# A batched A^T B^T matmul on one core: two-bank PSUM copies, no engine block, and the last transposes moved between two halves of a matmul group

## The chip, the cores and the metric

The kernel runs on one core of a Trainium2 chip. The metric is device time in microseconds for one execution; lower is better. Times come from repeated runs of the same program, and a profile comes from one more execution, whose own time is given beside its span (the time from its first to its last recorded instruction).

## The reference

```python
batch, m, k, n = 16, 512, 512, 512
a: (batch, k, m) float32      b: (batch, n, k) float32
np.matmul(a.transpose(0, 2, 1), b.transpose(0, 2, 1)).astype(np.float32)
```

For each of 16 batches the output is A^T B^T, 512 x 512, in float32. Each batch reads 1 MiB of `a` and 1 MiB of `b` and writes 1 MiB of output.

## The kernel before

One batch is one step; there is no tiling over DRAM beyond that. Five engines run their own lists of instructions and meet only at semaphores.

**SyncE (SP)** issues every transfer, all into one queue, in an order written out by hand. In step `i` it issues the load of `b` (line 108), the load of `a` (line 111) and, five steps late (`LAG = 5`), the store of batch `i - 5` (line 123). There are four load buffers for each input and seven output buffers. The load of `b[i]` waits until PE has transposed batch `i - 4` (`turned`), the load of `a[i]` until the first matmul group of batch `i - 4` is done (`summed`), and the store of batch `j` until all groups of batch `j + 1` are done, because that implies that the copies of batch `j` are. The last two stores wait for the copies themselves through `oa_go` and `od_go` (line 122). At the end SP waits for all stores to land (line 125).

**VectorE (DVE)** casts `b` to bfloat16 (`cast`, line 145), moves the transposed `b` from PSUM to SBUF (`turn`, line 151; its source fills two PSUM banks) and copies output groups 0 and 2 from PSUM to SBUF (line 167). Its order inside a batch `i` is: `turn(i + 1)`, copy of group 0, `cast(i + 2)`, copy of group 2. In the last step but one it also does `turn` of the last batch and casts the second half of the last `a` (line 175).

**ScalarE (ACT)** casts `a` to bfloat16 (line 183) and copies output groups 1 and 3 (line 194).

**TensorE (PE)** transposes `b` (8 instructions a batch, line 78; pairs of bfloat16 values are moved as one float32) and does 16 matmuls a batch in four groups `rm` of four (line 90). Each group has its own PSUM bank `o_ps[rm]`, and each group waits until the copy of the same bank in the batch before is done:

```python
def steady(rm):
    take(pe, (od_go, oa_go)[rm % 2])
...
with pe.Fori(0, B // 2 - 1) as _i:
    turn(1)
    multiply(0, 0, steady)
    turn(0)
    multiply(1, 1, steady)
multiply(0, 0, steady)
turn(1)
pe.wait_ge(ac2_go, 1)
multiply(1, 1, last)
```

So batch `i + 1` is transposed ahead of the matmuls of batch `i`, except at the very end, where the transposes of batch 15 come behind all the matmuls of batch 14.

**GpSimd** builds the identity for the transposes and does nothing else.

All of this stands in an `nc.Block()` (line 99) inside a `tc.tile_critical()` (line 42). Each of the two closes with drains and semaphores over the engines.

Of the kernel before, what the change touches and what calls it, by code (L numbers as in the profile page):

```python
# [11 lines left out]
def kernel(  # L12
# [6 lines left out]
    nc = tc.nc  # L19
    P = 128  # L20
    B, K, M = a.shape
    _, N, _ = b.shape
    KO = K // P
    KJ = KO // 2
    MO = M // P
    NO = N // P
    assert B % 2 == 0

    f32 = mybir.dt.float32
    cdt = mybir.dt.bfloat16  # L30
# [3 lines left out]
    a_v = a.rearrange("b (ki ko) m -> b ki ko m", ko=KO)  # L34
    b_v = b.rearrange("b (ni no) k -> b ni no k", no=NO)
    out_v = out.rearrange("b (mi mo) n -> b mi mo n", mo=MO)

    LOADS = 4
    OUTS = 7
    LAG = 5  # L40

    with tc.tile_critical():  # L42
        sb = lambda name, shape, dt: ctx.enter_context(nc.sbuf_tensor(name, shape, dt))
        ps = lambda name, shape, dt: ctx.enter_context(nc.psum_tensor(name, shape, dt))
        sem = tc.alloc_semaphore
        a_sb = [sb(f"a_sb{s}", [P, KO, M], f32) for s in range(LOADS)]
        b_sb = [sb(f"b_sb{s}", [P, NO, K], f32) for s in range(LOADS)]
        o_sb = [sb(f"o_sb{s}", [P, MO, N], f32) for s in range(OUTS)]
        a_bf = [sb(f"a_bf{s}", [P, KO, M], cdt) for s in range(2)]
# [1 line left out]
        bt_sb = [sb(f"bt_sb{s}", [P, KJ, N], f32) for s in range(2)]  # L51
        identity = sb("identity", [P, P], f32)
        bt_ps = [ps(f"bt_ps{s}", [P, KJ, NO, P], f32) for s in range(2)]
        o_ps = [ps(f"o_ps{s}", [P, N], f32) for s in range(MO)]


        a_in = [sem(f"a_in{s}") for s in range(LOADS)]
# [2 lines left out]
        turned = sem("turned")  # L60
# [4 lines left out]
        bt_go = sem("bt_go")  # L65
        ac_go = sem("ac_go")
        ac2_go = sem("ac2_go")
        oa_go = sem("oa_go")
        od_go = sem("od_go")

        def transposes(pe, x, y):

            w = b_bf[x][:].bitcast(f32).rearrange("p no (pk j) -> p no j pk", j=KJ)
            for j in range(KJ):
                for no in range(NO):
                    last = pe.transpose(bt_ps[y][:, j, no, :], w[:, no, j, :], identity[:])  # L78
            last.then_inc(turned, 1)

        def take(pe, s):
            pe.wait_ge(s, 1).then_inc(s, -1)  # L82

        def matmuls(pe, x, y, waits):
            a_r = a_bf[x][:].rearrange("p rk (pm rm) -> p rk rm pm", rm=MO)
            bt_h = bt_sb[y][:].bitcast(cdt).rearrange("p j (n h) -> p j h n", h=2)
            for rm in range(MO):
                waits(rm)
                for rk in range(KO):
                    last = pe.matmul(  # L90
                        o_ps[rm][:],
                        a_r[:, rk, rm, :],
                        bt_h[:, rk // 2, rk % 2, :],
                        start=(rk == 0),
                        stop=(rk == KO - 1),
                    )
                last.then_inc(summed, 1)

        with nc.Block() as block:

            @block.sync
            def _(sp):
                for i in range(B + LAG):
                    s, use = i % LOADS, i // LOADS
                    if i < B:
                        if use:
                            sp.wait_ge(turned, i - LOADS + 1)
                        sp.dma_start(b_sb[s][:], b_v[i]).then_inc(b_in[s], 16)
                        if use:
                            sp.wait_ge(summed, MO * (i - LOADS) + 1)  # L110
                        sp.dma_start(a_sb[s][:], a_v[i]).then_inc(a_in[s], 16)
                    j = i - LAG
                    if j >= 0:


                        if j + 2 < B:
                            sp.wait_ge(summed, MO * (j + 2))
                        else:

                            sp.wait_ge(summed, MO * (B - 1))  # L120
                            for s in (oa_go, od_go):
                                sp.wait_ge(s, 2 * (j + 3 - B))
                        sp.dma_start(out_v[j], o_sb[j % OUTS][:]).then_inc(o_out[j % OUTS], 16)
                for s in range(OUTS):
                    sp.wait_ge(o_out[s], 16 * len(range(s, B, OUTS)))

            @block.gpsimd
            def _(pool):
                pool.memset(identity[:], 0.0).then_inc(id_go, 1)  # L129
                pool.wait_ge(id_go, 1)  # L130
                pool.affine_select(  # L131
                    out=identity[:],
                    in_=identity[:],
                    compare_op=mybir.AluOpType.not_equal,
                    fill=1.0,
                    base=0,
                    pattern=[[-1, P]],
                    channel_multiplier=1,
                ).then_inc(id_go, 1)

            @block.vector
            def _(dve):
                def cast(i):
                    dve.wait_ge(b_in[i % LOADS], 16 * (i // LOADS + 1))
                    dve.tensor_copy(b_bf[i % 2][:], b_sb[i % LOADS][:]).then_inc(bc_go, 1)  # L145

                def turn(i):


                    dve.wait_ge(turned, i + 1)  # L150
                    dve.tensor_copy(  # L151
                        bt_sb[i % 2][:].rearrange("p j (ni no) -> p j ni no", no=NO),
                        bt_ps[i % 2][:].rearrange("p j no ni -> p j ni no"),
                    ).then_inc(bt_go, 1)

                dve.sem_inc(od_go, 2)
                cast(0)
                cast(1)
                turn(0)
                for i in range(B):  # L160
                    if i + 2 < B:
                        turn(i + 1)
                    if i >= OUTS:
                        dve.wait_ge(o_out[i % OUTS], 16 * (i // OUTS))
                    for rm in (0, 2):
                        dve.wait_ge(summed, MO * i + rm + 1)
                        dve.tensor_copy(o_sb[i % OUTS][:, rm, :], o_ps[rm][:]).then_inc(od_go, 1)  # L167
                        if rm == 0 and i + 2 < B:
                            cast(i + 2)
                    if i + 2 == B:  # L170
                        turn(i + 1)

                        s = (i + 1) % LOADS
                        dve.wait_ge(a_in[s], 16 * ((i + 1) // LOADS + 1))
                        dve.tensor_copy(  # L175
                            a_bf[(i + 1) % 2][:, KO // 2:, :], a_sb[s][:, KO // 2:, :]
                        ).then_inc(ac2_go, 1)

            @block.scalar
            def _(act):  # L180
                def cast(i, part=slice(None)):
                    act.wait_ge(a_in[i % LOADS], 16 * (i // LOADS + 1))
                    act.copy(a_bf[i % 2][:, part, :], a_sb[i % LOADS][:, part, :]).then_inc(ac_go, 1)  # L183

                act.sem_inc(oa_go, 2)
                cast(0)
                for i in range(B):
                    if i + 2 < B:
                        cast(i + 1)
                    if i >= OUTS:  # L190
                        act.wait_ge(o_out[i % OUTS], 16 * (i // OUTS))
                    for rm in (1, 3):
                        act.wait_ge(summed, MO * i + rm + 1)
                        act.copy(o_sb[i % OUTS][:, rm, :], o_ps[rm][:]).then_inc(oa_go, 1)  # L194
                    if i + 2 == B:
                        cast(i + 1, slice(0, KO // 2))

            @block.tensor
            def _(pe):
                def steady(rm):  # L200
                    take(pe, (od_go, oa_go)[rm % 2])

                def last(rm):
                    pe.wait_ge((od_go, oa_go)[rm % 2], 1 + rm // 2)

                def multiply(x, y, waits):
                    take(pe, bt_go)
                    take(pe, ac_go)
                    matmuls(pe, x, y, waits)

                def turn(x):
                    take(pe, bc_go)
                    transposes(pe, x, x)

                pe.wait_ge(id_go, 2)
                turn(0)
                with pe.Fori(0, B // 2 - 1) as _i:
                    turn(1)
                    multiply(0, 0, steady)
                    turn(0)  # L220
                    multiply(1, 1, steady)
                multiply(0, 0, steady)
                turn(1)
                pe.wait_ge(ac2_go, 1)
                multiply(1, 1, last)


# [28 lines left out]
```

## Time and profile before

| | |
|---|---|
| time, median of 5 runs | 127.54 us (126.79 to 128.37) |
| the profiled execution's own time | 126.82 us |
| its span | 124.9 us |
| mean granted TensorE clock | 0.926 |
| PE matmul busy | 87.4 us, 70% of the span |
| DVE busy | 59.3 us, 48% |
| ACT busy | 49.2 us, 39% |
| DMA | 50.35 MB, 403 GB/s over the span |

The table is read as shares of the span. The busy time of PE is an upper figure, since matmuls are pipelined. The transfer row counts what all 16 DMA engines moved for this core. 1.9 us of the execution's own time lie outside its span. Which of these rows sets the time is a matter of the stages, not of the shares alone.

### The profile page before, as it was taken

The numbers are of one execution on the slowest core, as the hardware profiler recorded it, in microseconds if no ns is written. First come the engines' busy times: TensorE is split into PE (matmuls) and PEld (weight loads), VectorE is DVE, ScalarE is ACT, GpSimd is POOL, SyncE is SP. The second block draws the span as 40 slices with busy tenths as digits, with TensorE's granted clock in tenths as the row PEclk, the third lists the DMA queues.
The fourth block names the chain that finished last, engine by engine and source line by source line (L and its number), as shares of the span: only waits on it lengthen the run. The fifth ranks groups of instructions, "written<-read, shape, count | busy, mean of one in ns | idle before, by whom it ended". The sixth has DMA issues, their size and how long they took to land. (4 is left out here: it accounts for less than half of the span.)

```text
span 124.9 us, 1151 instructions
## 1 busy us (share of the span) xinstructions
PE 87.4 (70%) x384; PEld 48.4 (39%) x384; DVE 59.3 (48%) x65; ACT 49.2 (39%) x49; POOL 0.7 (1%) x6
## 2 busy tenths in 40 slices
PE   0061999999991997839696591988749699549800
PEld 0051646656641535335262441435244364233200
DVE  0125666696655627255470745627156561762200
ACT  4032617467561625506353161625505362140300
POOL 2000000000000000000000000000000000000000
PEclk9999999999999689986999999689986999996897
DMA  2999999999999999999999999999999999999981
GB/s 68 425 428 420 425 422 425 420 428 415 357 428 425 422 433 420 428 420 430 428 422 415 436 428 430 425 420 425 428 430 430 422 417 425 428 433 428 407 359 52
DMA packets 6914, 50.35 MB, mean 403 GB/s; under 512 B 768, under 2 KB 768, under 8 KB 768
## 3 DMA queue, kind: packets, MB, share of 16 engines
q1 hardware_dynamic: 6912, 50.33, 96.4%
q14 instruction: 2, 0.02, 0.1%
HBM read 33.55 MB, written 16.78 MB: 403 GB/s over the span
## 5 line engine op out<-in xcount | busy, mean ns | idle before, releaser
L90 PE MATMUL o_ps<-bt_sb,a_bf 128*128 128x512 bf16 x256 | 69.1, 427 | 3.4 <-PEq L82 3.4
L90 PEld LDWEIGHTS o_ps<-bt_sb,a_bf 128*128 128x128 bf16 x256 | 30.5, 120 | 36.7 <-issue 15.5
L183 ACT CAST a_bf<-a_sb 128x2048 bf16<-128x2048 f32 (+1 forms) x16 | 29.6, 1847 | 30.6 <-DMA a_sb<-in_a_dram 30.5
L78 PE MATMUL bt_ps<-identity,b_bf 128*128 128x128 f32 x128 | 21.5, 320 | 27.2 <-PEq L82 27.2
L145 DVE CAST b_bf<-b_sb 128x2048 bf16<-128x2048 f32 x16 | 19.6, 1224 | 36.0 <-DMA b_sb<-in_b_dram 36.0
L194 ACT COPY o_sb<-o_ps 128x512 f32<-128x512 f32 x32 | 18.7, 586 | 37.9 <-PE o_ps L90 37.4
L78 PEld LDWEIGHTS bt_ps<-identity,b_bf 128*128 128x128 f32 x128 | 18.9, 211 | 32.5 <-issue 31.7
L151 DVE COPY bt_sb<-bt_ps 128x1024 f32<-128x1024 f32 x16 | 19.6, 1224 | 14.8 <-PE bt_ps L78 14.8
L167 DVE COPY o_sb<-o_ps 128x512 f32<-128x512 f32 x32 | 21.8, 684 | 7.7 <-PE o_ps L90 7.7
L183 ACT ACT_TABLE_LOAD x1 | 1.3, 1283 | 1.0 <-SPq L42 1.0
L175 DVE CAST a_bf<-a_sb 128x1024 bf16<-128x1024 f32 x1 | 0.7, 683 | 0.0
L131 POOL TENSOR_SCALAR_AFFINE_SELECT identity<-identity 128x128 f32<-128x128 f32 x1 | 0.3, 292 | 0.2 <-POOL identity L129 0.2
L129 POOL MEMSET identity<- 128x128 f32 x1 | 0.2, 204 | 0.5 <-SPq L42 0.5
L240 POOL MEMSET const-bfloat16-1.0<- 128x1 bf16 x1 | 0.1, 101 | 0.0
L240 POOL MEMSET const-uint8-127<- 128x1 uint8 x1 | 0.1, 101 | 0.0
L240 POOL MEMSET const-float32-0.0<- 128x1 f32 x1 | 0.1, 98 | 0.2 <-issue 0.2
L240 POOL MEMSET const-float32-1.0<- 128x1 f32 x1 | 0.1, 98 | 0.0
## 6 DMA issues: line engine op xcount, KB each, us to landing
b_sb<-in_b_dram SPq DMA_DIRECT2D x16, 1024.0 KB, 18.7
a_sb<-in_a_dram SPq DMA_DIRECT2D x16, 1024.0 KB, 19.2
out_dram<-o_sb SPq DMA_DIRECT2D x16, 1024.0 KB, 18.6
```

The costliest lines, as they stand in the source:

```text
L78: last = pe.transpose(bt_ps[y][:, j, no, :], w[:, no, j, :], identity[:])
L90: last = pe.matmul(o_ps[rm][:], a_r[:, rk, rm, :], bt_h[:, rk // 2, rk % 2, :], start=(rk == 0), stop=(rk == KO - 1),)
L129: pool.memset(identity[:], 0.0).then_inc(id_go, 1)
L131: pool.affine_select(out=identity[:], in_=identity[:], compare_op=mybir.AluOpType.not_equal, fill=1.0, base=0, pattern=[[-1, P]], channel_ ...
L145: dve.tensor_copy(b_bf[i % 2][:], b_sb[i % LOADS][:]).then_inc(bc_go, 1)
L151: dve.tensor_copy(bt_sb[i % 2][:].rearrange("p j (ni no) -> p j ni no", no=NO), bt_ps[i % 2][:].rearrange("p j no ni -> p j ni no"),).then ...
L167: dve.tensor_copy(o_sb[i % OUTS][:, rm, :], o_ps[rm][:]).then_inc(od_go, 1)
L175: dve.tensor_copy(a_bf[(i + 1) % 2][:, KO // 2:, :], a_sb[s][:, KO // 2:, :]).then_inc(ac2_go, 1)
L183: act.copy(a_bf[i % 2][:, part, :], a_sb[i % LOADS][:, part, :]).then_inc(ac_go, 1)
L194: act.copy(o_sb[i % OUTS][:, rm, :], o_ps[rm][:]).then_inc(oa_go, 1)
L240: nc = _bacc.Bacc("TRN2", target_bir_lowering=False, num_devices=1)
```

## The change

Four things change together.

1. The four one-bank output tensors become two tensors of two banks, `o_ps[0]` for groups 0 and 1 and `o_ps[1]` for groups 2 and 3. In batches 0 to 14 DVE copies the first pair in one instruction and ACT the second pair in one. In the last batch each group is still copied alone. PE waits once a half, not once a group.
2. DVE's order in a batch becomes `turn(i + 1)`, copy of both groups of the first half, `cast(i + 2)`.
3. The `nc.Block()` is gone; each engine's list is written straight into the critical section, in plain functions.
4. At the end, the transposes of batch 15 stand between the two halves of batch 14's matmuls. DVE copies the first half of batch 14 ahead of the `turn` of batch 15, and ACT casts its half of the last `a` ahead of its copy of batch 14.

The store of batch `j` now waits for three of the four groups of batch `j + 1`.

```diff
-        o_ps = [ps(f"o_ps{s}", [P, N], f32) for s in range(MO)]
+        o_ps = [ps(f"o_ps{s}", [P, MO // 2, N], f32) for s in range(2)]
...
-        with nc.Block() as block:
...
-                            sp.wait_ge(summed, MO * (j + 2))
+                    sp.wait_ge(summed, MO * (j + 1) + 3)
...
-                            for s in (oa_go, od_go):
-                                sp.wait_ge(s, 2 * (j + 3 - B))
+                    sp.wait_ge(od_go, 1 if j + 2 == B else 3)
+                    sp.wait_ge(oa_go, 1 if j + 2 == B else 3)
...
+        def copy_out(eng, i, rm):
+            s = i % OUTS
+            q = rm if isinstance(rm, int) else rm.stop - 1
+            if s != i:
+                eng.wait_ge(o_out[s], 16 * (i // OUTS))
+            eng.wait_ge(summed, MO * i + q + 1)
...
+            copy(o_sb[s][:, rm, :], o_ps[h][:, p, :]).then_inc(go, 1)
...
+            for i in range(B - 2):
+                turn(i + 1)
+                copy_out(dve, i, slice(0, 2))
+                cast(i + 2)
+            copy_out(dve, B - 2, slice(0, 2))
+            turn(B - 1)
+            cast_a(dve, B - 1, slice(KO // 2, KO)).then_inc(ac2_go, 1)
+            copy_out(dve, B - 1, 0)
+            copy_out(dve, B - 1, 2)
...
+            for i in range(B - 2):
+                cast_a(act, i + 1, slice(None)).then_inc(ac_go, 1)
+                copy_out(act, i, slice(2, 4))
+            cast_a(act, B - 1, slice(0, KO // 2)).then_inc(ac_go, 1)
+            copy_out(act, B - 2, slice(2, 4))
+            copy_out(act, B - 1, 1)
+            copy_out(act, B - 1, 3)
...
+            def half(x, h, wait):
...
+                wait((od_go, oa_go)[h])
+                for q in range(2):
+                    for rk in range(KO):
+                        last = pe.matmul(
+                            o_ps[h][:, q, :],
...
+                    last.then_inc(summed, 1)
...
+            take(bt_go)
+            take(ac_go)
+            half(0, 0, take)
+            turn(1)
+            half(0, 1, take)
+            pe.wait_ge(ac2_go, 1)
+            take(bt_go)
+            take(ac_go)
+            half(1, 0, lambda s: pe.wait_ge(s, 1))
+            half(1, 1, lambda s: pe.wait_ge(s, 1))
```

The loop over batches 0 to 13 on PE keeps its order: `turn(1)`, `multiply(0)`, `turn(0)`, `multiply(1)`.

More of the change, by code (lines that the diff above doesn't have):

```diff
@@ L67 @@
         ac2_go = sem("ac2_go")
+        od_go = sem("od_go")
         oa_go = sem("oa_go")
[L69 to L116, printed above, removed]
-                            sp.wait_ge(summed, MO * (j + 2))
-                        else:
-                            sp.wait_ge(summed, MO * (B - 1))
-                            for s in (oa_go, od_go):
[L122 to L158, printed above, removed]
-                turn(0)
[L160 to L225, printed above, removed]
@@ new lines, in run_sp, with load, store @@
+        def run_sp(sp):
+            def load(i):
+                s, use = i % LOADS, i // LOADS
+                if use:
+                    sp.wait_ge(turned, i - LOADS + 1)
+                sp.dma_start(b_sb[s][:], b_v[i]).then_inc(b_in[s], 16)
+                if use:
+                    sp.wait_ge(summed, MO * (i - LOADS) + 1)
+                sp.dma_start(a_sb[s][:], a_v[i]).then_inc(a_in[s], 16)
+            def store(j):
+                if j + 2 < B:
+                    sp.wait_ge(summed, MO * (j + 1) + 3)
+                else:
+                    sp.wait_ge(summed, MO * (B - 1))
+                    sp.wait_ge(od_go, 1 if j + 2 == B else 3)
+                    sp.wait_ge(oa_go, 1 if j + 2 == B else 3)
+                sp.dma_start(out_v[j], o_sb[j % OUTS][:]).then_inc(o_out[j % OUTS], 16)
+            for i in range(B + LAG):
+                if i < B:
+                    load(i)
+                if i >= LAG:
+                    store(i - LAG)
+            for s in range(OUTS):
+                sp.wait_ge(o_out[s], 16 * len(range(s, B, OUTS)))
@@ new lines, in run_pool, with cast_a @@
+        def run_pool(pool):
+            pool.memset(identity[:], 0.0).then_inc(id_go, 1)
+            pool.wait_ge(id_go, 1)
+            pool.affine_select(
+                out=identity[:],
+                in_=identity[:],
+                compare_op=mybir.AluOpType.not_equal,
+                fill=1.0,
+                base=0,
+                pattern=[[-1, P]],
+                channel_multiplier=1,
+            ).then_inc(id_go, 1)
+        def cast_a(eng, i, part):
+            s = i % LOADS
+            eng.wait_ge(a_in[s], 16 * (i // LOADS + 1))
+            copy = eng.copy if eng is nc.scalar else eng.tensor_copy
+            return copy(a_bf[i % 2][:, part, :], a_sb[s][:, part, :])
@@ new lines, in copy_out @@
+        def copy_out(eng, i, rm):
[4 more added lines that the diff above has]
+            eng.wait_ge(summed, MO * i + q + 1)
+            copy = eng.copy if eng is nc.scalar else eng.tensor_copy
+            h = q // 2
+            p = rm - 2 * h if isinstance(rm, int) else slice(None)
+            go = oa_go if eng is nc.scalar else od_go
+            copy(o_sb[s][:, rm, :], o_ps[h][:, p, :]).then_inc(go, 1)
@@ new lines, in run_dve, with cast, turn @@
+        def run_dve(dve):
+            def cast(i):
+                dve.wait_ge(b_in[i % LOADS], 16 * (i // LOADS + 1))
+                dve.tensor_copy(b_bf[i % 2][:], b_sb[i % LOADS][:]).then_inc(bc_go, 1)
+            def turn(i):
+                dve.wait_ge(turned, i + 1)
+                dve.tensor_copy(
+                    bt_sb[i % 2][:].rearrange("p j (ni no) -> p j ni no", no=NO),
+                    bt_ps[i % 2][:].rearrange("p j no ni -> p j ni no"),
+                ).then_inc(bt_go, 1)
+            dve.sem_inc(od_go, 1)
+            cast(0)
+            cast(1)
+            turn(0)
+            for i in range(B - 2):
[7 more added lines that the diff above has]
+            copy_out(dve, B - 1, 2)
@@ new lines, in run_act, with run_pe, take, turn @@
+        def run_act(act):
+            act.sem_inc(oa_go, 1)
+            cast_a(act, 0, slice(None)).then_inc(ac_go, 1)
+            for i in range(B - 2):
[5 more added lines that the diff above has]
+            copy_out(act, B - 1, 3)
+        def run_pe(pe):
+            def take(s):
+                pe.wait_ge(s, 1).then_inc(s, -1)
+            def turn(x):
+                take(bc_go)
+                w = b_bf[x][:].bitcast(f32).rearrange("p no (pk j) -> p no j pk", j=KJ)
+                for j in range(KJ):
+                    for no in range(NO):
+                        last = pe.transpose(bt_ps[x][:, j, no, :], w[:, no, j, :], identity[:])
+                last.then_inc(turned, 1)
+            def half(x, h, wait):
+                a_r = a_bf[x][:].rearrange("p rk (pm rm) -> p rk rm pm", rm=MO)
+                bt_h = bt_sb[x][:].bitcast(cdt).rearrange("p j (n h) -> p j h n", h=2)
+                wait((od_go, oa_go)[h])
[3 more added lines that the diff above has]
+                            o_ps[h][:, q, :],
+                            a_r[:, rk, 2 * h + q, :],
+                            bt_h[:, rk // 2, rk % 2, :],
+                            start=(rk == 0),
+                            stop=(rk == KO - 1),
+                        )
+                    last.then_inc(summed, 1)
+            def multiply(x):
+                take(bt_go)
+                take(ac_go)
+                half(x, 0, take)
+                half(x, 1, take)
+            pe.wait_ge(id_go, 2)
+            turn(0)
+            with pe.Fori(0, B // 2 - 1) as _i:
+                turn(1)
+                multiply(0)
+                turn(0)
+                multiply(1)
+            take(bt_go)
+            take(ac_go)
+            half(0, 0, take)
+            turn(1)
+            half(0, 1, take)
+            pe.wait_ge(ac2_go, 1)
+            take(bt_go)
+            take(ac_go)
+            half(1, 0, lambda s: pe.wait_ge(s, 1))
+            half(1, 1, lambda s: pe.wait_ge(s, 1))
@@ L229 @@
+        run_sp(nc.sync)
+        run_pool(nc.gpsimd)
+        run_dve(nc.vector)
+        run_act(nc.scalar)
+        run_pe(nc.tensor)
 _INS = ['a', 'b']
```

## The prediction

> **What bounds the kernel now.** I read the page's rows of slices first, then the waits of SP, then the end in order of time, then the transfer share in half microseconds. The page:
>
> ```profile
> PEclk9999999999999689986999999689986999996897
> DMA  2999999999999999999999999999999999999981
> GB/s 68 425 428 420 425 422 425 420 428 415 357 428 425 422 433 420 428 420 430 428 422 415 436 428 430 425 420 425 428 430 430 422 417 425 428 433 428 407 359 52
> ```
>
> Slices are 3.12 us. From slice 1 to slice 37 the DMA share is 9 throughout and the rate about 427 GB/s, whatever PE's clock does above it. 50.33 MB at 427 GB/s are 117.9 us of the 124.9 us span. So the transfers are the bound, and only 7.0 us are not steady transfer: slice 0 (about 2.6 us until data flow), one dip in slice 10 (357 instead of 427, 0.5 us), and the end. A gain has to come out of these.
>
> SP's waits say how far the queue runs ahead:
>
> ```profile
> SPq L123 <- PE o_ps L90: 47.1, 14, 8.6
> SPq L111 <- PE o_ps L90: 38.0, 12, 6.3
> SPq L122 <- ACT o_sb L194: 8.3, 2, 8.0
> ...
> SPq L125 <- DMA out_dram<-o_sb: 4.0, 1, 4.0
> ```
>
> SP waits long for PE, yet the DMA engines never run dry, because a transfer lands a median 18.6 to 19.2 us after its issue (part 6 of the page), while the quickest needed 4.5 us. Some 14 us of every transfer are queueing; a batch is 3.15 MB, 7.37 us at 427 GB/s. Compute may come 14 us later, or any amount earlier, without moving a byte in the middle. The third line is the exception: SP stood 8.0 us in front of the last store. The end in order of time:
>
> ```profile
> 105.66 1.23 DVE L145 CAST b_bf<-b_sb 128x2048 bf16<-128x2048 f32 x1 [2.94 <-DMA b_sb<-in_b_dram]
> ...
> 106.81 1.28 DVE L167 COPY o_sb<-o_ps 128x512 f32<-128x512 f32 x2
> ...
> 107.63 1.99 PE L90 MATMUL o_ps<-bt_sb,a_bf 128*128 128x512 bf16 x8 [1.32 <-PEq L82]
> ...
> 109.46 1.11 PE L78 MATMUL bt_ps<-identity,b_bf 128*128 128x128 f32 x8
> ...
> 111.75 0.68 DVE L175 CAST a_bf<-a_sb 128x1024 bf16<-128x1024 f32 x1
> ...
> 112.69 5.39 PE L90 MATMUL o_ps<-bt_sb,a_bf 128*128 128x512 bf16 x16 [2.12 <-PEq L82]
> ...
> 118.11 0.58 ACT L194 COPY o_sb<-o_ps 128x512 f32<-128x512 f32 x1 [1.52 <-PE o_ps L90]
> ```
>
> The last batch is a serial chain: `b` lands, cast, a copy of batch 13 that stood behind that cast, second half of batch 14's matmuls, transposes, `turn`, half cast of `a`, 16 matmuls, copy. SP then issues the last store at 118.77. Did the queue wait for it? Stretches of half a microsecond; the last three numbers of a line are the granted clock, the DMA share and GB/s:
>
> ```profile
> 118.50:119.00 0.50, 0.00 (x0) 0.00 (x0) 0.00 (x0) 0.20 (x1) 0.00 (x0) 1.00 0.58 246
> 119.00:119.50 0.50, 0.00 (x0) 0.00 (x0) 0.00 (x0) 0.00 (x0) 0.00 (x0) 1.00 0.47 197
> 119.50:120.00 0.50, 0.00 (x0) 0.00 (x0) 0.00 (x0) 0.00 (x0) 0.00 (x0) 1.00 1.15 459
> 120.00:120.50 0.50, 0.00 (x0) 0.00 (x0) 0.00 (x0) 0.00 (x0) 0.00 (x0) 1.00 0.74 311
> ```
>
> Yes, a little. Summed over 118.0 to 120.5, with the share before of 0.93, the lost share is 0.5 x (0.07 + 0.42 + 0.53 - 0.15 + 0.26) = 0.57 us for the mean DMA engine. Data of the last store flow from 119.5, 0.7 us after its issue, and the store lands with the end of SP's 4.0 us wait, at 123.25. Drains follow until 124.9.
>
> **Part 1: the copies.** DVE replaces two copies of 684 ns by one of two banks. The nearest row is line 151, 1224 ns for 128x1024 out of two banks, though read in steps: bounds 1224 and 1368, I take 1224, 0.14 us less a batch. ACT has no two-bank row: its casts, 1901 ns for 2048 elements and 1047 for 1024, give 0.83 ns an element, so 586 + 512 x 0.83 = 1.01 us (bounds 586 ns and 2 x 586). Both lie beside the transfers: 0 us on the total.
>
> Against the merging speaks the Trainium skill, Perfetto Trace Analysis, Optimizing Scalar/DVE Operations: where these engines aren't saturated but cause bubbles elsewhere, smaller instructions let work finish sooner. DVE is at 48%. Today `cast(i + 2)` starts behind one group's matmuls and one copy; afterwards behind two groups and 1.22 us. PE's loop becomes half a batch's matmuls (8 x 234 ns = 1.87, from 24 in 5.62 us at 100.69), copy 1.22, cast 1.23, transposes 1.20: 5.5 us, against 16 x 234 ns + 1.20 = 4.9 us when PE alone sets it. By the rule that is 0.6 us a batch, 14 x 0.6 = 8 us. By the trace it is nothing, since 5.5 is below 7.37. I take nothing. In return, group 2 no longer waits for a copy queued behind the cast's wait for `b`.
>
> **Part 2: SP.** A store waits for one group less, so it and the load of `b` listed behind it are issued up to a microsecond or two earlier; with 14 us of queueing this is 0. The order in the queue is unchanged, and no transfer is added.
>
> **Part 3: no block.** It removes the block's closing round:
>
> ```profile
> L99 SPq COMPARE_BRANCH  x1: 33/33/33, 123.3 to 123.3; - x1
> L99 SPq DRAIN  x1: 7/7/7, 123.4 to 123.4; - x1
> L99 SPq EVENT_SEMAPHORE  x1: 17/17/17, 123.6 to 123.6; - x1
> ```
>
> SP's wait ends at 123.25 and the critical section's own closing (line 42) begins at 123.67: 0.42 us, on the path, with no cover. Some decoding stays, so I take 0.35; bounds 0.42, and 0 if the next closing round takes over the wait. At the start the one branch of SP (0.8 us) belongs to line 251, outside the block, and the first load is issued at 0.94: I take 0, at most 0.1.
>
> **Part 4: the end.** I rebuild it with the durations above. DVE copies batch 13's first half at 102.6 and then waits for `b`, which still lands at 105.64; cast until 106.9. PE has done batch 14's first half by about 106.3, because its copies (DVE 103.8, ACT 105.5) are early. Transposes 106.95 to 108.15; second half to 110.0. DVE meanwhile: copy 106.9 to 108.1, `turn` to 109.4, half cast to 110.1. Behind that `turn` on DVE stands only the half cast, behind ACT's half cast (from 108.1, when `a` has landed) only batch 14's second copy, at 110.0 to 111.0, for which PE's last half waits without loss. Batch 15's matmuls: 110.2 to 113.9 warm, copy to 114.5, store issued near 114.6, 4.2 us earlier.
>
> The clock matters here. The Trainium skill (TensorE: Matmul & The Clock Gate, HAM oscillation) wants no PE gaps above about 3.4 us. The trace is stricter: only 2.12 us of idle stood before the last 16 matmuls, and yet
>
> ```profile
> 114.00:115.00 1.00, 1.00 (x4) 0.42 (x3) 0.68 (x1) 0.00 (x0) 0.00 (x0) 0.50 0.95 401
> ```
>
> half the clock was granted. By the rule the new end is warm, 3.7 us; by the trace it can be 5.4, and 16 x 427 ns = 6.8 at worst, which puts the store at 117.7. The fastest engines run dry at about 118.5 and data need 0.7 us, so the deadline is 117.8. All three meet it.
>
> What is late next is the queue itself. Filling the gap saves between 0 (if the engine that lands last never stood still; from 122.0 to 123.0 the shares are 0.17 and less, so few engines set the end) and 0.57 us. About half of them stood still: I take 0.40.
>
> **Sum.** 126.82 - 0.40 - 0.35 = 126.07 against the profiled execution, 0.6% less. The runs shown have the median 127.54, above that execution; the same share gives **126.8 us**.
>
> **Rivals.**
> - *Hidden anyway* (126.82 again, 127.5 on the median): the slow DMA engines set the end, and the section's own closing absorbs the block's. For it: few engines are busy after 122. Against: SP's 0.42 us are plainly serial.
> - *All of it and more* (faster): gap 0.57, closing 0.42, start 0.1, and the dip of slice 10 (0.5) doesn't recur: 126.82 - 1.59 = 125.23, on the median 125.9. For it: nothing in the queue explains that dip, so it may be chance. Against: it falls in the time of the first store's data, which stay where they are.
> - *PE and DVE in step at half clock* (slower): the longer dependence breaks PE's work into pieces with idle between, and the clock stays at 0.50. Place: the 14 batches of the loop. Price: 16 x 427 ns + 8 transposes, 1.95 us cold = 8.8 us a batch, 1.4 above 7.37. It decides once the 14 us of queueing are used up, after 10 such batches running; 14 of them give 20 - 14 = 6 us, about 133. Against it: PEclk falls to 6 only in single slices, and between them warm batches give back 1.8 us each.
>
> **Chances.** Forecast 0.62, more than it 0.16, hidden 0.15, half clock 0.07. What a measurement of this kernel can tell from no change is about 1%. Of the forecast 0.04 lie beyond that, of "hidden" 0.02 on the slow side: faster 0.20, same 0.71, slower 0.09. The range goes from 125.9, all bounds together, to 127.9: "hidden" at 127.5 and 0.4 for the spread of the runs (126.79 to 128.37). Half clock lies outside.
>
> **What would show it.** Right: the last store issued between 114 and 118 and no fall of the DMA share before about 121; line 99's rows gone and some 0.35 us less from the last landing to the end; 30 copies fewer (15 on DVE, 15 on ACT), DVE's merged ones near 1.22 us and ACT's near 1.0; the GB/s row unchanged. Wrong: a GB/s row that sags in mid-run (PE's loop too long), a last store still behind 118, a closing as long as before, or a first load later than 0.94.

## The result, and the profile after

The changed kernel takes 126.66 us (median of 42 runs, 126.06 to 127.56), the kernel before 127.0 us (median of 79 runs). The ratio is 0.9966, with a 95% interval of 0.9953 to 0.9979: 0.43 us less (0.0034 x 127.0), where the forecast had 0.75. It is inside 1%, so by the measure of the prediction it is the same. The two profiled executions took nearly the same time, 126.82 us before and 126.85 after, so the profiles below show what moved, and the medians show the gain.

The page of the changed kernel, the same rows as shown of before: PE's granted clock, the mean share of the DMA engines, and what they moved, in slices of 3.12 us.

```profile
PEclk9999999999999999999999959996799999999965
DMA  3999999999999999999999999999999999999991
GB/s 60 423 434 431 423 420 420 423 420 426 370 426 420 426 420 428 426 423 428 420 428 428 426 426 428 426 415 436 397 426 428 423 420 436 431 423 426 423 389 42
...
q14 instruction: 1, 0.01, 0.0%
```

The picture is that of before: full from slice 1 to slice 37, the same dip in slice 10, one more small one in slice 28. The last line counts loads of code, which come over the same DMA engines; before, there were two.

SP's waits, then the end in order of time:

```profile
SPq L81 <- PE o_ps L195: 50.5, 12, 6.3
SPq L93 <- PE o_ps L195: 35.0, 15, 7.0
SPq L101 <- DMA out_dram<-o_sb: 7.3, 1, 7.3
SPq L92 <- ACT o_sb L133: 4.9, 2, 3.2
```

```profile
106.20 1.23 DVE L138 CAST b_bf<-b_sb 128x2048 bf16<-128x2048 f32 x1 [1.65 <-DMA b_sb<-in_b_dram]
107.34 1.22 DVE L133 COPY o_sb<-o_ps 128x1024 f32<-128x1024 f32 x1
...
107.57 1.19 PE L186 MATMUL bt_ps<-identity,b_bf 128*128 128x128 f32 x8 [0.73 <-PEq L176]
...
108.60 1.98 PE L195 MATMUL o_ps<-bt_sb,a_bf 128*128 128x512 bf16 x8
...
110.88 3.80 PE L195 MATMUL o_ps<-bt_sb,a_bf 128*128 128x512 bf16 x16 [0.30 <-PEq L176]
...
114.77 0.59 ACT L133 COPY o_sb<-o_ps 128x512 f32<-128x512 f32 x1 [1.23 <-PE o_ps L195]
```

The chain at the end runs as the prediction rebuilt it: copy of both first groups, transposes between the halves, 16 matmuls warm. SP waits at most 3.2 us for the copies of a last store where it waited 8.0, issues the last store at 115.45 instead of 118.77, and then waits 7.3 us for it to land instead of 4.0. The two waits have changed places. What the DMA engines did meanwhile, in half microseconds; the last two numbers are the DMA share and GB/s:

```profile
118.50:119.00 0.50, 0.00 (x0) 0.00 (x0) 0.00 (x0) 0.00 (x0) 0.00 (x0) 1.00 1.09 459
119.00:119.50 0.50, 0.00 (x0) 0.00 (x0) 0.00 (x0) 0.00 (x0) 0.00 (x0) 1.00 0.93 393
...
121.00:121.50 0.50, 0.00 (x0) 0.00 (x0) 0.00 (x0) 0.00 (x0) 0.00 (x0) 0.50 0.82 344
121.50:122.00 0.50, 0.00 (x0) 0.00 (x0) 0.00 (x0) 0.00 (x0) 0.00 (x0) 0.50 0.31 131
122.00:122.50 0.50, 0.00 (x0) 0.00 (x0) 0.00 (x0) 0.00 (x0) 0.00 (x0) 0.50 0.23 98
122.50:123.00 0.50, 0.00 (x0) 0.00 (x0) 0.00 (x0) 0.00 (x0) 0.00 (x0) 0.50 0.08 33
```

The gap at 118.5 to 119.5 is filled, and yet the last landing is at 123.28, where it was at 123.23 (both from the trace's landing events, one for each of the 16 parts of a transfer, one part to a DMA engine). What was saved in the gap is idle again behind 121.5: most engines now end early and few go on. Before, two of the same stretches read:

```profile
121.50:122.00 0.50, 0.00 (x0) 0.00 (x0) 0.00 (x0) 0.00 (x0) 0.00 (x0) 1.00 1.06 442
122.00:122.50 0.50, 0.00 (x0) 0.00 (x0) 0.00 (x0) 0.00 (x0) 0.00 (x0) 1.00 0.17 66
```

The 16 parts of the last store land between 121.25 and 123.28; before, between 122.44 and 123.23.

The end of the program, read from the critical section's own closing (its records; the first start is in tenths):

```profile
L42 SPq EVENT_SEMAPHORE  x3: 17/28/28, 123.5 to 123.7; - x3
...
L78 SPq COMPARE_BRANCH  x1: 33/33/33, 123.3 to 123.3; - x1
```

SP's wait ends at 123.30 and the closing begins at 123.50: 0.20 us, where it was 0.42. A branch of SP stands in this stretch before and after (before it was put down to the block's line 99, now, in the second line, to line 78); the rest of the block's round is gone.

### The profile page after: what moved, and what is told of

The parts are those of the page before. It is cut to its first block, busy times and chain, and to the rows that moved or that the text cites. A ratio compares the mean times of both kernels' runs of the same rounds, so it can differ in the third digit from the quotient of the medians.

```text
span 124.7 us, 1082 instructions
## 1 busy us (share of the span) xinstructions
PE 83.5 (67%) x384; PEld 46.8 (37%) x384; DVE 58.9 (47%) x50; ACT 46.7 (37%) x34; POOL 0.7 (1%) x6
## 5 line engine op out<-in xcount | busy, mean ns | idle before, releaser
L195 PE MATMUL o_ps<-bt_sb,a_bf 128*128 128x512 bf16 x256 | 64.6, 406 | 0.3 <-PEq L176 0.3
L195 PEld LDWEIGHTS o_ps<-bt_sb,a_bf 128*128 128x128 bf16 x256 | 29.8, 117 | 29.6 <-issue 6.3
L186 PEld LDWEIGHTS bt_ps<-identity,b_bf 128*128 128x128 f32 x128 | 18.2, 211 | 37.8 <-issue 37.8
L133 ACT COPY o_sb<-o_ps 128x1024 f32<-128x1024 f32 (+1 forms) x17 | 16.4, 963 | 39.7 <-PE o_ps L195 39.7
L133 DVE COPY o_sb<-o_ps 128x1024 f32<-128x1024 f32 (+1 forms) x17 | 19.7, 1161 | 15.5 <-PE o_ps L195 15.5
```

What stands on the lines that cost most here:

```text
L133: copy(o_sb[s][:, rm, :], o_ps[h][:, p, :]).then_inc(go, 1)
L186: last = pe.transpose(bt_ps[x][:, j, no, :], w[:, no, j, :], identity[:])
L195: last = pe.matmul(o_ps[h][:, q, :], a_r[:, rk, 2 * h + q, :], bt_h[:, rk // 2, rk % 2, :], start=(rk == 0), stop=(rk == KO - 1),)
```

## The experiments

Two theories stood at the start. **Gap**: the idle of the DMA engines in front of the last store costs time, 0.2 to 0.4 us, and the block's round 0.2 us more. **Laggard**: the DMA engine that is furthest behind sets the end, it never stood idle, so the moment of the last store is free up to some point, and the gain is the block's round and something else. Each ratio below is to the kernel before, run on the same chip, from 12 runs (5 for the one with added code).

**The last store late again.** ACT does two more casts ahead of its last copy.

```diff
             copy_out(act, B - 1, 1)
+            act.wait_ge(summed, MO * B)
+            act.copy(a_bf[0][:], a_sb[0][:])
+            act.copy(a_bf[1][:, 0:3, :], a_sb[1][:, 0:3, :])
             copy_out(act, B - 1, 3)
```

> The changed kernel with two added casts on ACT (1.9 and 1.5 us, into buffers that nobody reads any more) ahead of the last copy, so that the last store is issued at about 118.8 as in the kernel before. If the gap in front of the last store costs time, it comes back: DMA share under 0.6 at 118.5 to 119.5, and 0.2 us (what is left of the gain beside the closing) to 0.4 us (the forecast's term) above the changed kernel. If lagging DMA engines set the end anyway, the share falls but the last landing and the time stay within 0.1 us of the changed kernel.

The store is issued at 118.49. Ratio 0.9969 (0.9949 to 0.9989); the changed kernel has 0.9966. The gap came back in part, and the time did not:

```profile
118.50:119.00 0.50, 0.00 (x0) 0.00 (x0) 0.00 (x0) 0.00 (x0) 0.00 (x0) 1.00 0.74 311
119.00:119.50 0.50, 0.00 (x0) 0.00 (x0) 0.00 (x0) 0.00 (x0) 0.00 (x0) 1.00 0.82 344
```

That speaks for the laggard, though the interval reaches 0.25 us to either side.

**The transposes behind again.**

```diff
             half(0, 0, take)
-            turn(1)
             half(0, 1, take)
+            turn(1)
...
-            cast_a(act, B - 1, slice(0, KO // 2)).then_inc(ac_go, 1)
             copy_out(act, B - 2, slice(2, 4))
+            cast_a(act, B - 1, slice(0, KO // 2)).then_inc(ac_go, 1)
```

> The changed kernel with the transposes of batch 15 behind all matmuls of batch 14 again, and ACT's half cast of the last a behind its copy of batch 14. If the move of the transposes is what brought the last store forward, the store goes back to 118 or later and 0.2 us are lost. The rival: what held it back was DVE's copy of batch 13 behind the cast, which parts 1 and 2 removed; then the store is issued at 116.5 to 117.8, still ahead of the point at which the DMA engines run dry, and the time is that of the changed kernel (ratio 0.9966).

The last store is issued at 119.21, later than before the change: the move of the transposes is what brings it forward; ACT's half cast, moved with it, was done at 112.04, ahead of DVE's at 112.80, and held nothing up (the last 16 matmuls took 5.39 us, with half the clock granted, as before). The rival about DVE's copy is wrong. But the ratio is 0.9968 (0.9946 to 0.9990), no loss. Its shares in half microseconds show why:

```profile
119.00:119.50 0.50, 0.00 (x0) 0.00 (x0) 0.00 (x0) 0.12 (x1) 0.00 (x0) 1.00 0.50 213
119.50:120.00 0.50, 0.00 (x0) 0.00 (x0) 0.00 (x0) 0.00 (x0) 0.00 (x0) 1.00 0.43 180
...
121.50:122.00 0.50, 0.00 (x0) 0.00 (x0) 0.00 (x0) 0.00 (x0) 0.00 (x0) 0.50 1.01 410
122.00:122.50 0.50, 0.00 (x0) 0.00 (x0) 0.00 (x0) 0.00 (x0) 0.00 (x0) 0.50 0.94 393
122.50:123.00 0.50, 0.00 (x0) 0.00 (x0) 0.00 (x0) 0.00 (x0) 0.00 (x0) 0.50 0.02 0
```

For a whole microsecond half of the engines' time or more is idle, and then all work and end together: the 16 parts land within 0.18 us, the last at 123.08. The early engines had time to lose. In the landing events, the last part of the last store comes 2.41 us behind the last part of the store ahead of it, which is one store at full rate: the laggard had no gap at all.

**Later still.** Four added casts and copies on ACT, 5.9 us by their rows.

```diff
+            act.copy(a_bf[0][:], a_sb[0][:])
+            act.copy(a_bf[1][:], a_sb[1][:])
+            act.copy(bt_sb[0][:], a_sb[2][:, 0:2, :])
+            act.copy(bt_sb[1][:], a_sb[2][:, 2:4, :])
             copy_out(act, B - 1, 3)
```

> The changed kernel with 5.9 us of added casts and copies on ACT (into buffers that nobody reads any more) ahead of the last copy: the last store is issued near 121.4 us. With the store at 118.5 and at 119.2 nothing was lost. If the DMA engine that lags most sets the end, the store now is behind even that one: it lands 3.9 us after its issue (what the run with the store at 119.2 took), near 125.3, and the time rises by 2.0 us against the changed kernel (ratio 1.012). If the store's lateness were not on the path at all, the ratio would stay at 0.9966; if it cost one for one from the forecast's deadline of 117.8, it would rise by 3.6 us (1.025).

Issued at 121.04, landed at 124.88, 3.84 us later as expected. Ratio 1.0082 (1.0049 to 1.0115), 1.5 us above the changed kernel; at the store's real moment the laggard theory asks for 124.88 - (121.00 + 2.44) = 1.44, where 121.00 is the last landing of the store ahead and 2.44 one store. Between 120.5 and 121.5 next to nothing was started:

```profile
120.00:120.50 0.50, 0.00 (x0) 0.00 (x0) 0.00 (x0) 0.50 (x2) 0.00 (x0) 0.50 0.31 131
120.50:121.00 0.50, 0.00 (x0) 0.00 (x0) 0.00 (x0) 0.45 (x1) 0.00 (x0) 0.50 0.01 0
121.00:121.50 0.50, 0.00 (x0) 0.00 (x0) 0.00 (x0) 0.00 (x0) 0.00 (x0) 0.50 0.00 0
```

So the last store is free up to about 123.2 - 3.85 = 119.4 us, an estimate from its landing 3.84 to 3.87 us after its issue. The one run behind that point fits a cost of one for one.

**The block put back, and the block alone taken away.**

```diff
-        run_sp(nc.sync)
...
+        with nc.Block() as block:
+            block.sync(run_sp)
+            block.gpsimd(run_pool)
...
```

> The changed kernel with the block put back round the same engine lists. If the closing round is a serial cost, the stretch from the end of SP's last wait to the critical section's own closing goes back from 0.20 us to 0.42 us and the time rises by 0.2 us against the changed kernel (ratio to the kernel before about 0.998). If the section's own closing absorbs it, the stretch stays at 0.2 and the ratio at 0.9966. The last store is issued at about 115.5 in either case.

The stretch is 0.42 us again (122.95 to 123.37), the ratio 0.9979 (0.9960 to 0.9998). The direction and the size (0.17 us) fit a serial cost; against 0.9966 the intervals overlap.

In the kernel before, the functions of the four engines and SP were written without the block, nothing else changed:

```diff
-        with nc.Block() as block:
-
-            @block.sync
-            def _(sp):
+        def run_sync(sp):
...
+        run_sync(nc.sync)
```

> The kernel before with the block alone taken away. Closing stretch 0.20 instead of 0.42 us, last store still at about 118.8, ratio 0.998 if the closing is serial. If the missing block is all that the change gains (the gap in front of the last store being hidden by the DMA engines that lag), the ratio is that of the whole change, 0.9966.

The stretch fell to 0.19 us (123.75 to 123.94), but the ratio is 1.0010 (0.9985 to 1.0035): no gain seen. Two things in its profile stood against it. A load of code came in the closing itself, at 125.3, and from the closing's start to the end it took 1.38 us instead of 1.21 to 1.23, so 0.16 of the 0.23 us went there. And its slowest DMA engine was further behind than in any other profile with this amount of code (the store ahead of the last landed over 2.41 us, until 121.28); 0.6 us of that came in one step, from 66.40 to 69.45 us, where no load of code stands.

**The kernel before, again.**

> The kernel before, unchanged, as one of the kernels compared: what the comparison gives where there is no difference (ratio 1.000 within 0.002), and a second profile of it. In the first one the last store landed 2.81 us behind the one ahead of it, against 2.41 to 2.45 in every other profile, and a code-loading transfer of 8 KB stood at 119.8 us, between the two. If code loading at that moment is what costs the 0.37 us, both come again; if the late last store does, the 2.81 comes again without it; if neither, the step is 2.45.

Ratio 1.0001 (0.9966 to 1.0037): this is what no change looks like. The second profile has the last store at 119.15, the load of code at 120.1, 752 ns long, and the last store landing 3.00 us behind the one ahead of it. So the kernel before does lose 0.4 to 0.6 us at the very end in both of its profiles, with a store that is no later than the harmless one above (119.21). Its 16 parts land from 122.82 to 123.72.

The packets of both traces say where this time went. In each, 15 of the 16 parts of the last store land by 122.85 and 123.19 us, 2.43 and 2.47 behind the store ahead, which is one store at full rate: the laggard lost nothing. One part comes 0.38 and 0.53 us later. The records do not name the engine of a packet, but their times do: the load of code (119.77 us for 692 ns; 120.14 for 752) is followed without a gap by eight packets of the store, and these end at 122.91 and 123.34, when all the others had ended by 122.38 and 122.86. So a load of code held one engine back, after the late store had put all of them near the end together. In the changed kernel the load near the end (117.66 us, 309 ns, the data packet behind it 655 ns instead of 309) fell on an engine that had room: its data ended at 121.69, those of the last engine at 122.93.

**The copies split again.**

```diff
-            copy(o_sb[s][:, rm, :], o_ps[h][:, p, :]).then_inc(go, 1)
...
+                copy(o_sb[s][:, 2 * h, :], o_ps[h][:, 0, :])
+                copy(o_sb[s][:, 2 * h + 1, :], o_ps[h][:, 1, :]).then_inc(go, 1)
```

> The changed kernel with each two-bank copy split into two copies of one bank, everything else (order, waits, end) as changed. DVE and ACT have 15 instructions more each. If the gain that the block and the tail do not explain (0.2 us) comes from the shorter programs (a code-loading transfer of 8 KB near 99 us is in the profiles of the programs with one-bank copies and not in those with two-bank copies), that transfer comes back and the ratio rises from 0.9966 to 0.998 or more. If it comes from the copies' time, 0.06 us on DVE and 0.16 us on ACT a batch, hidden under the transfers, nothing changes: 0.9966.

The load of code near 99 us came back (99.8), and a second one at 119.1: the added instructions bring them. The ratio, 0.9977 (0.9945 to 1.0009), is between the two answers and its interval holds both. Undecided.

**Added code.**

```diff
             ).then_inc(id_go, 1)
+            for c in range(1024):
+                pool.memset(spare[:, c : c + 1], 0.0)
```

> The changed kernel with 1024 tiny memsets on GpSimd, which is idle otherwise, into a buffer that nobody reads: some 8 more loads of 8 KB of code, about 100 us of GpSimd time off every path. If a load of code delays the DMA engine that carries it by its own 0.31 us, and one engine carries them all, the last landing falls behind by up to 8 x 0.31 = 2.5 us (less by what that engine is ahead of the slowest one, up to 2 us); spread over the engines it is 0.3 us or less. If code loading is no matter, the time stays within 0.1 us of the changed kernel.

Ratio 1.0305 (1.0243 to 1.0368), 4.3 us above the changed kernel, although GpSimd is done at 41.4 us. The page has nine loads of code, eight of them between 6.9 and 42.1 us, and the rate falls away only at the end:

```profile
GB/s 87 411 426 421 426 424 429 411 424 370 414 409 424 424 414 424 426 426 424 426 426 419 434 421 429 424 426 429 429 426 431 424 429 429 421 350 431 299 181 10
...
q14 instruction: 9, 0.07, 0.2%
```

One store's parts land over 5.6 us in the second half of this run, over 2.0 in the changed kernel: a single DMA engine has fallen behind. In the landing events the last part of a transfer comes 3.13 to 3.16 us after that of the one ahead in four of the eight steps with a load of code, and some 2.48 where none stands, so such a load costs the engine that carries it some 0.65 us, twice what its packet lasts (0.31). The packets show the other half: the data packet behind the load lasts 660 ns instead of 309. (The other four steps were 2.96, 3.00 and 3.08, and 3.71 with a load of 706 ns at the time of the first store.) Eight times 0.65 make 5.2 us; the end moved by 3.6 us in the profile (126.90 against 123.28), the rest being what this engine had been ahead of the laggard. The expectation had the kind right and the price at half.

**A longer list for ACT.** The late store of the first experiment once more, and ACT's list brought to the length it had before:

```diff
             act.sem_inc(oa_go, 1)
+            act.wait_ge(id_go, 2)
+            for c in range(13):
+                act.copy(spare[:, c : c + 1], identity[:, c : c + 1])
```

> The changed kernel with the late last store (118.5 us, two added casts ahead of ACT's last copy, into buffers that nobody reads any more) and 13 tiny copies at the start of ACT's list, where ACT is idle, so that ACT's list is as long as in the kernel before. In both profiles of the kernel before, a load of code stood between the last two stores (119.8 and 120.1 us, 692 and 752 ns) and the last store landed 2.81 and 3.00 us behind the one ahead of it; in the profile with the same late store and the short ACT list, and in all others, the step was 2.39 to 2.45 (but for the store at 121.0). If the length of ACT's list brings the load there and the load delays the DMA engine that carries it, a load comes between 118.5 and 120.5, the step is 2.7 or more, and the time rises by 0.3 to 0.5 us against the run with the late store alone (ratio from 0.997 to about 1.000). If it is not ACT's code or the load does no harm, the step is 2.45 and the ratio 0.997.

A second load of code did come, so the length of ACT's list brings it, but at 117.9, 309 ns long, ahead of the last store's data (issued at 117.91). The step to the last landing was 2.42 us, the ratio 0.9958 (0.9936 to 0.9981). No harm: a second load near the end is not enough. Whether it has to fall between the last two stores, as in both profiles of the kernel before, is not answered by this run. Loads at 118.9 to 120.1 us in three other runs (transposes behind, copies split, added code) left the step at 2.41 to 2.45.

**The first store earlier, a tiny one ahead of all, and two queues at the start.** These look at what else is idle: the dip near 32 us and the slow start.

```diff
-    LAG = 5
+    LAG = 4
```

> The changed kernel with stores issued four steps behind the loads instead of five, so that the data of the first store move some 5 us earlier (from about 33 us to about 28 us). The dip of the transfer rate at 31 to 34 us (0.4 to 0.55 us lost) moves with it to about 26 to 29 us if the first store causes it, and stays if it is tied to the time or to chance. The total stays within 0.2 us.

The dip moved with the first store, from slice 10 to slice 8 (339, where the changed kernel has 420); ratio 0.9964 (0.9933 to 0.9994).

```profile
GB/s 66 415 431 428 428 425 420 425 339 436 399 425 425 420 428 410 428 428 425 420 428 433 418 420 423 433 428 428 428 420 428 425 428 431 423 428 425 423 386 58
```

```diff
+            act.wait_ge(f_go, 1)
+            act.dma_start(out_v[0][:, 0, 0:4], first[:]).then_inc(f_out, 16)
             act.sem_inc(oa_go, 1)
```

> The changed kernel with one tiny store (16 bytes a partition, later overwritten by the true output) issued from ACT's queue near 1.2 us, while the first loads are on their way. The dip of 0.3 to 0.55 us moved with the first store when that came earlier. If it is a cost of the first write alone, it is paid now in the first 3 us, where the DMA engines wait for data anyway; the dip at 31 to 34 us goes, and the time falls by up to 0.4 us (ratio 0.993). If it belongs to loads and full stores running side by side, the dip and the time stay (0.9966).

Ratio 0.9974 (0.9946 to 1.0003): no gain in time. Slice 10 has 394, which is within what that slice varies by (357 to 417 in the kernels with this order of stores), so the dip is not shown to be any smaller.

```diff
-                sp.dma_start(a_sb[s][:], a_v[i]).then_inc(a_in[s], 16)
+                if i:
+                    sp.dma_start(a_sb[s][:], a_v[i]).then_inc(a_in[s], 16)
...
+            act.dma_start(a_sb[0][:], a_v[0]).then_inc(a_in[0], 16)
             act.sem_inc(oa_go, 1)
```

> The changed kernel with the first load of a issued from ACT's queue at the same moment as the first load of b from SP's, so that seven later loads are issued 0.44 us earlier. If the slow start of the transfers (data from 2.0 us, full rate from 3.0 us) comes from SP's issuing one load after the other, up to 0.3 us are gained (ratio 0.994). If it is the time that the first data take to come, nothing (0.9966).

Ratio 0.9951 (0.9923 to 0.9978), the lowest here, but its interval holds 0.9966, and its start was not faster: the four half microseconds from 2.0 to 4.0 us have 66, 229, 246 and 344 GB/s, those of the changed kernel 147, 98, 393 and 442. So issuing the first loads earlier, from two queues, did not make the start faster, and this version is not shown to beat the changed kernel.

## Why the prediction was right or wrong, point by point

**The bound** held: the transfers run at full rate throughout, and the longer loop of PE and DVE cost nothing (the GB/s row), where the rule on smaller instructions would have had 8 us. Merged copies took 1.22 to 1.23 us on DVE and 1.01 on ACT, as estimated. The loop is seen where the stores first follow it: stores 2 to 4 were issued at 29.45, 35.01 and 40.56 us, 5.56 apart, and before at 28.62, 33.20 and 37.79, 4.58 apart (forecast 5.5 and 4.9).

**Part 2**, SP, had the time right and the direction there wrong: these stores came up to 2.8 us later, not earlier. The queueing covered it.

**Part 3**, the block, was taken at 0.35 us. It measured 0.22, since one branch of SP is left: 0.42 to 0.20 in the closing, 0.42 again with the block put back. In the time it shows in one direction (0.9979 against 0.9966, with intervals that overlap) and not in the other (1.0010), where a load of code in the closing took 0.16 of it.

**Part 4**, the end, was right in its steps on the engines: the store was forecast for 114.6 and came at 115.45, of which 0.54 us is that `b` landed later (106.18 for 105.64). The step that failed is the price: "About half of them stood still: I take 0.40". For the store's moment alone it is 0 within what 12 runs can tell (0.9969 and 0.9968 against 0.9966). The sum counted the mean engine's idle, and the end belongs to the engine that is furthest behind. The 0.57 itself was loose: it counts from a share of 1.00, not from the 0.93 that stands beside it, which gives 0.39, and continued to 121.0, where the share is 1.19, it is 0.47. The bound of 0 stood in the prediction with the right reason, and was not taken. The deadline failed with it: 117.8 was when the fastest engines run dry; by the runs it is about 119.4, when the slowest does. That 126.66 lies so near to the forecast 126.8 is luck in part: the gain was 0.43 us instead of 0.75, and the median of the kernel before fell from 127.54 (5 runs) to 127.0 (79).

**The clock.** The last 16 matmuls were warm, 3.80 us. But "the trace is stricter" was read from one gap: in the same profile 2.68 us of idle, at 70.1 us, were followed by 16 matmuls in 3.80 us.

**The rivals.** "Hidden anyway" was right about the gap and, by the closing's own records, wrong about the block. The half clock came in two spells of 3.4 us, not in ten batches running. "It may be chance", said of the dip in the faster rival, has one run against it, in which the dip came with the earlier first store. Its depth is not fixed: with the first store in its old place, slice 10 had 405 and 417 in two runs (the store at 121.04, two queues).

**What stays open.** 0.22 us of the 0.43 are the closing. The other 0.2 us are not the idle of the mean engine in the gap. Both profiles of the kernel before lose 0.37 and 0.56 us between the last two stores (steps of 2.81 and 3.00 us against 2.44) through one load of code on one engine, and no profile of the changed kernel or of its variants does; the one longer step among these belongs to the store issued at 121.04. That would cover it, so the earlier store may be worth the room that it leaves for such a load. That this makes the medians differ is argued and not shown: the run that brought a second load near this place did not bring the loss back, and the kernel without the block alone, whose profile has no load there, was no faster (1.0010). What sets the moment of a load is open too. The intervals of 12 runs reach 0.2 to 0.4% to either side, more than the 0.2 us asked for.

## What to carry to other kernels

Where transfers are the bound, look at the end engine by engine: idle of the mean DMA engine is not time unless the engine that lands last is idle too, and the spread of one transfer's landings says how much room the others have. When one part lands alone, look in the packets for what its engine carried. Delaying a suspect by a known amount, once a little and once too much, gives its deadline more surely than any sum. A serial round at the end is worth what it measures in the closing, less what remains of its code.

## What the runs showed of the hardware

A load of code goes through the same DMA engines as the data, and one of 0.31 us set the engine that carried it back by about 0.65 us, so a long list on otherwise idle GpSimd cost 4.3 us in all. At the end of the kernel before, one load cost 0.4 to 0.5 us. The 16 parts of one 1 MiB transfer, equal shares of it, land over 0.2 to 0.9 us in the first 25 us and over 1.4 to 2.4 us just ahead of the last store (without added code): the DMA engines drift apart, mostly about the first stores. About the first store's data up to 0.6 us of the transfer rate were lost, at both places tried. And 2.12 us of idle were followed by half the clock on PE in two programs, the kernel before and the one with the transposes behind, while 2.68 us in the kernel before (at 70.1 us) and 2.54 in the changed one (at 100.2) were followed by the full clock: here the length of one gap did not decide it.
